# A transformer block on one core: side transfers on GpSimd's queue, and a first norm that spreads repeated columns into two banks

## The chip, the cores and the metric

The kernel runs on one NeuronCore of a Trainium2 chip. The metric is the device time of one execution in microseconds. Each core has a tensor engine (TensorE) for matrix products, a vector engine (VectorE), a scalar engine (ScalarE), GpSimd and SyncE; every engine takes its own instructions in order and waits on semaphores. Transfers between memory (DRAM) and the on-chip buffer (SBUF) run on 16 DMA engines; an instruction on SyncE, ScalarE or GpSimd issues them. TensorE writes to PSUM banks, which VectorE and ScalarE read.

## The reference

One block over 512 tokens of 1024 features, all in float32. A vector c gives six vectors of 1024 (adaLN) through a matrix `w_mod`:

```python
mod = (c_act @ w_mod[l] + b_mod[l])[:, None, :]        # c_act = silu(c)
shift_m, scale_m, gate_m, shift_f, scale_f, gate_f = jnp.split(mod, 6, axis=-1)
h = rms_norm(x, norm_mix[l]) * (1.0 + scale_m) + shift_m
z = h @ w_in[l]
qa, ka, va, xr, yr, qc, kc, vc, g_logits = jnp.split(z, IN_OFFSETS, axis=-1)
... # o_a: sliding-window attention, 8 heads; o_b: a gated linear recurrence (RG-LRU) times gelu(yr);
... # o_c: block-sparse attention (MoBA), 8 heads; both attentions add a bias by distance
merged = g[:, :, 0] * (o_a @ wb_a) + g[:, :, 1] * (o_b @ wb_b) + g[:, :, 2] * (o_c @ wb_c)
x = x + gate_m * (merged @ w_out[l])
h = rms_norm(x, norm_ffn[l]) * (1.0 + scale_f) + shift_f
u_gate, u_val = jnp.split(causal_dwconv(h @ w_up[l], ...), 2, axis=-1)
x = x + gate_f * ((jax.nn.silu(u_gate) * u_val) @ w_down[l])
```

## The kernel before

Features lie on the partitions: x is eight tiles of 128 features x 512 tokens (`X[0..7]`). Every large product is made in three passes of a reduced float32 format (float32r): a number is split into a high part and the exact rest, and high x high, high x low and low x high are added up (`mm3`). Weights arrive in chunks of 128x1024 (512 KB) in three buffers `raw`; ScalarE writes the high parts into `hi`, VectorE the rest into `lo` (`split`). TensorE then takes 24 products of a chunk.

The program is recorded, not issued at once. `Emitter` keeps, for each engine, a list of the instructions in the order of the code; `flush` (line 269) issues them at the end by a rough clock of its own. Up to the last of the first eight projections every engine's order is exactly the recorded one; behind that point each engine takes, among its next few instructions (`WINDOW`, line 49), the first whose operands the rough clock calls ready. The list `ORDER` (line 56) fixes the order of the later projections; between them TensorE takes up steps of side tasks: norms of heads, transposes, scores, the recurrence. Waits are put in from the operands. What is fixed at build time is each engine's order; if data come later than the rough clock thought, the engine waits there.

The prologue (lines 513 to 735). SyncE's queue loads `c8` and `CS` (c and an identity), the eight tiles of x, a table `V`, then w_mod and weights (`load_wm`, line 605; `stream_to`). TensorE spreads c over all partitions: for each half VectorE writes four diagonal blocks, and `spread` (line 593) multiplies them by ones. ScalarE squares the tiles of x, VectorE adds seven of them up; `token_ssq` (line 570) sums over the features by products with a column of ones, which gives a token per partition. `warm` (line 631) issues products whose result nobody reads. `rsqrt_sqrt` (line 576) makes the inverse root by a root on ScalarE and one Newton step on VectorE; `spread_diag` (line 586) writes its diagonals, half on each of the two engines, and two products by ones put 1/rms of all tokens on every partition, in one bank `rbk`. `mod_col` (line 609) makes a column of an adaLN vector: 128 features, the dot product of w_mod's rows with c on VectorE. `norm_in` (line 685) then makes h: for tile 0 from the bank, in two halves of the tokens, for the others from a copy `rb` in SBUF; the high part is written by ScalarE (`Hh`), the rest by VectorE (`Hl`). The first eight projections run f = 0..7 over the tiles of h, into eight banks at once.

Later, SyncE's queue carries everything else as well: rows of the attention bias out to DRAM and a tile for each head back (`bias_rows`, line 748; `bias_tile`, line 763), copies of k to the other half of the partitions (`turn_task`, line 803), 32 loads of w_mod (`mod_task`, line 998), gate weights (line 1055), gates out to DRAM and back (lines 1157, 1205), and x once more (`x_task`, line 1183). An instruction that waits in a queue holds all that is behind it. A weight load waits until the buffer `raw` that it fills has been split. `lru_task` (line 1065) writes the first column of a tile by a memset on GpSimd.

Of the kernel before, what the change touches and what calls it, by code (L numbers as in the profile page):

```python
# [10 lines left out]
F32 = mybir.dt.float32  # L11
# [3 lines left out]
OP = mybir.AluOpType  # L15
AX = mybir.AxisListType

S = 512
# [7 lines left out]
# Columns of the per-feature vectors ("vec" input): feature f of a vector sits at partition f % 128,  # L26
# column f // 128 of its range.
# [8 lines left out]
# Columns of the shape-only constants ("cst" input).  # L36
# [7 lines left out]
# from the end of an instruction to the start of one that needs it  # L44
DELAY = {("pe", "pe"): 0.0, ("act", "act"): 0.13, ("dve", "dve"): 0.13, ("act", "dve"): 0.145, ("act", "pe"): 0.27,
         ("dve", "act"): 0.14, ("dve", "pe"): 0.256, ("pe", "act"): 0.197, ("pe", "dve"): 0.2}
# What steers the order of issue. WINDOW: how many instructions of an engine are looked at; SLACK: how much later
# than the first ready one a longer one may start, in us; NEAR, BACKLOG, LIMIT: when the side tasks' steps are taken up.
WINDOW = {"pe": 160, "act": 45, "dve": 45, "dma": 6, "pool": 4}
SLACK, NEAR, BACKLOG, LIMIT = 1.2, 2, 8, 2  # L50
# how many heads are in flight, and how many up-projections start on the first half of the tokens
FLY, FIRST = 4, 5
# The order of the projections: qk, vc, xr, yr; m: the rest of the adaLN vectors may start; g, h: a branch's gates
# ahead of their use (swa, moba); a, b, c: the branches (swa, rg-lru, moba) into the merge. "-": no side tasks in
# between.
# [5 lines left out]
class Buf:  # L61
    """A tile that is used again and again; Tile orders its uses, the emitter picks the ones that are free."""
# [21 lines left out]
class Emitter:  # L84
    """Emits instructions engine by engine and keeps a rough clock of each engine, so that the tensor engine's
    stream takes up work of the side tasks when its operands are there. The order it picks is one of many right
    ones: Tile puts in every wait."""
# [15 lines left out]
    # clocks  # L103
    @staticmethod
    def keys(ap):
        """What an operand touches: the tile, or the 256 columns of a slot."""
# [73 lines left out]
    # instructions  # L180
# [68 lines left out]
    def sums(self, out, a):  # L249
        """out[:, h] = the sum of a[:, h, :]."""  # L250
        self._go("dve", 0.067 + self.n(a) * 0.00104, [out], [a], lambda: self.nc.vector.tensor_reduce(
            out, a, axis=AX.X, op=OP.add))
# [10 lines left out]
    def dma(self, out, in_, kb=256):  # L263
        self._go("dma", kb / 370, [out], [in_], lambda: self.nc.sync.dma_start(out, in_))  # L264
        for k in self.keys(out):
            self.w[k] += 2.0

    # the order of issue
# [1226 lines left out]
```

## Time and profile before

| what | value |
|---|---|
| time, median of 3 runs | 905.96 us (905.86 to 906.26) |
| profiled execution, first to last instruction | 904.7 us |
| TensorE busy | 895.8 us (99%) |
| VectorE busy | 630.1 us (70%) |
| ScalarE busy | 475.3 us (53%) |
| GpSimd busy | 1.8 us (0%) |
| DMA, mean over the span | 146 GB/s, 131.70 MB, all program transfers on one queue |

The profile is of one execution; its rows are times from the span's start. "PE" is TensorE, "PEld" its loads of weights, "DVE" VectorE, "ACT" ScalarE, "POOL" GpSimd, "SP" SyncE. Matrix products are pipelined and their ends are modelled, so that busy time alone does not tell whether TensorE is at its best rate; the distance from one start to the next does. A float32 product shows as two records. A line number is that of the helper which records the operation (L187 is every product, L213 every ScalarE operation), so that groups are told apart by the names of their tiles.

### The profile page before, as it was taken

What the parts mean: (1) busy time and instruction counts of PE and PEld (TensorE: products, weight loads), DVE (VectorE), ACT (ScalarE), POOL (GpSimd) and SP (SyncE); (2) the same over time, 40 slices, a digit from 0 to 9 for tenths busy, and PEclk for the clock granted to TensorE, in tenths of its full rate; (3) what the DMA queues carried; (4) which work ended last, traced back from release to release, by engine and by line L of the source; (5) the groups of instructions that cost most, each with busy time, mean ns of one, the idle gap of its engine ahead of it and who ended that gap; (6) DMA issues with size and microseconds to landing.
All of it is one profiled execution on the core that took longest, in us unless ns stands there. A gap on an engine that the chain in (4) does not pass through costs nothing.

```text
span 904.7 us, 12494 instructions
## 1 busy us (share of the span) xinstructions
PE 895.8 (99%) x4730; PEld 772.0 (85%) x4730; DVE 630.1 (70%) x1138; ACT 475.3 (53%) x763; POOL 1.8 (0%) x15
## 2 busy tenths in 40 slices
PE   7999999999999999999999999999999999999998
PEld 6889989889888888878888999888888888888888
DVE  6989989997876875887676888766656665522321
ACT  5366767985875898732223566544444444321110
POOL 0000000000000000000000000000000000000000
PEclk9999999999999999999999999999999999999999
DMA  8933532442254244586667655333222223333320
GB/s 315 347 119 99 155 99 93 129 163 95 73 172 155 90 140 152 184 275 214 229 226 285 213 173 172 123 101 107 97 93 93 93 97 103 104 116 105 117 82 24
DMA packets 44286, 131.70 MB, mean 146 GB/s; under 512 B 5393, under 2 KB 6937, under 8 KB 44226
## 3 DMA queue, kind: packets, MB, share of 16 engines
q1 hardware_dynamic: 44226, 130.90, 43.2%
q8 instruction: 37, 0.61, 0.3%
q14 instruction: 23, 0.19, 0.1%
HBM read 122.46 MB, written 5.80 MB: 142 GB/s over the span
## 4 chain that ended last, share of the span: by engine, by line
PE 93%; ACT 3%; DVE 2%; issue 1%; DMA 0%; SPq 0%; POOLq 0%; POOL 0%; ACTq 0%
PE bank L187 91%; PE bank L191 2%; ACT pair L213 2%; ACT L213 1%; DMA pair<-in_xT_dram 0%; DVE pair L243 0%; DVE pair L240 0%; DVE pair L246 0%; DVE lo L240 0%; ACT hi L213 0%; ACT rslot L213 0%; DVE rslot L240 0%; DVE pair L258 0%; SPq L264 0%; DVE rslot L243 0%
## 5 line engine op out<-in xcount | busy, mean ns | idle before, releaser
L187 PE MATMUL bank<-rslot,hi 128*128 128x512 f32 (+1 forms) x2332 | 656.8, 367 | 0.4 <-ACT rslot L213 0.4
L187 PEld LDWEIGHTS bank<-rslot,hi 128*128 128x128 f32 x2332 | 419.7, 189 | 70.1 <-ACT rslot L213 0.8
L187 PE MATMUL bank<-rslot,lo 128*128 128x512 f32 (+1 forms) x1166 | 427.0, 367 | 0.0
L240 DVE TENSOR_TENSOR lo<-raw,hi 128x1024 fp32r<-128x1024 f32 (+1 forms) x169 | 197.7, 1171 | 151.7 <-ACT hi L213 150.3
L213 ACT ACTIVATE hi<-raw 128x1024 fp32r<-128x1024 f32 (+1 forms) x153 | 156.6, 1025 | 185.3 <-PE bank L187 164.1
L187 PEld LDWEIGHTS bank<-rslot,lo 128*128 128x128 f32 x1166 | 219.9, 189 | 35.8
L187 PE MATMUL bank<-hi,rslot 128*128 128x256 f32 (+1 forms) x448 | 92.0, 315 | 0.1
L243 DVE SCALAR_TENSOR_TENSOR pair<-bank,V,pair 128x511 f32<-128x511 f32 (+2 forms) x112 | 83.6, 746 | 2.8 <-ACT pair L213 1.1
L187 PEld LDWEIGHTS bank<-hi,rslot 128*128 128x128 f32 x448 | 74.3, 190 | 6.3 <-issue 0.9
L213 ACT ACTIVATE rslot<-pair 128x512 fp32r<-128x512 f32 (+2 forms) x60 | 37.2, 622 | 76.7 <-DVE pair L240 72.6
L246 DVE CUSTOM_DVE_ANT_0 pair<-pair,pair,V 128x1024 f32<-128x1024 f32 x48 | 61.1, 1280 | 11.5 <-DMA pair<-in_wm_dram 11.5
L213 ACT ACTIVATE pair<-bank,V 128x512 f32<-128x512 f32 (+1 forms) x84 | 61.5, 732 | 4.8 <-PE bank L187 4.1
L213 ACT ACTIVATE pair<-bank 128x512 f32<-128x512 f32 (+2 forms) x75 | 43.2, 611 | 39.2 <-PE bank L187 38.6
L187 PE MATMUL bank<-lo,rslot 128*128 128x256 f32 (+1 forms) x224 | 62.5, 315 | 0.0
L213 ACT ACTIVATE pair<-pair 128x512 f32<-128x512 f32 (+1 forms) x62 | 35.2, 572 | 47.1 <-DVE pair L243 45.2
L240 DVE TENSOR_TENSOR rslot<-pair,rslot 128x512 fp32r<-128x512 f32 (+2 forms) x67 | 45.5, 680 | 15.2 <-ACT rslot L213 14.7
L240 DVE TENSOR_TENSOR pair<-pair,pair 128x512 f32<-128x512 f32 (+1 forms) x72 | 45.6, 636 | 12.6 <-ACT pair L213 7.6
L213 ACT ACT_TABLE_LOAD x37 | 47.5, 1283 | 5.2 <-PE bank L187 3.8
L187 PE MATMUL bank<-rslot,rslot 128*128 128x256 f32 (+3 forms) x288 | 48.8, 309 | 0.0
L187 PEld LDWEIGHTS bank<-rslot,rslot 128*128 128x128 f32 x288 | 43.4, 189 | 4.7 <-DVE rslot L240 0.8
L213 ACT ACTIVATE pair<-pair,small 128x256 f32<-128x256 f32 (+3 forms) x78 | 40.4, 529 | 11.3 <-DVE small L234 10.3
L187 PEld LDWEIGHTS bank<-lo,rslot 128*128 128x128 f32 x224 | 42.7, 190 | 2.6
(76 smaller groups left out, 412.5 us busy)
## 6 DMA issues: line engine op xcount, KB each, us to landing
raw<-in_wz_dram SPq DMA_DIRECT2D x50, 512.0 KB, 3.8
raw<-in_wup_dram SPq DMA_DIRECT2D x49, 512.0 KB, 3.3
pair<-in_wm_dram SPq DMA_DIRECT2D x48, 512.0 KB, 5.5
raw<-in_wdn_dram SPq DMA_DIRECT2D x22, 512.0 KB, 3.3
raw<-in_wout_dram SPq DMA_DIRECT2D x16, 512.0 KB, 3.3
pair<-in_xT_dram SPq DMA_DIRECT2D x16, 256.0 KB, 5.4
raw<-in_w_dram SPq DMA_DIRECT2D x8, 512.0 KB, 5.5
raw<-in_wbr_dram SPq DMA_DIRECT2D x16, 256.0 KB, 3.0
```

Source lines behind the costliest of these rows:

```text
L187: self._go("pe", cost, [out], [lhsT, rhs], lambda: self.nc.tensor.matmul(out, lhsT, rhs, start=start, stop=stop), rows=lhsT.shape[0] / 128)
L191: self._go("pe", 0.107, [out], [in_, ident], lambda: self.nc.tensor.transpose(out, in_, ident))
L213: self._go("act", c, outs, ins, lambda: self.nc.scalar.activation(out, in_, func, scale=scale, **kw), "tanh" if func == AF.Tanh else t)
L240: self._dve([out], [a, b], lambda: self.nc.vector.tensor_tensor(out, a, b, op=op))
L243: self._dve([out], [a, s, b], lambda: self.nc.vector.scalar_tensor_tensor(out, a, s, b, op0=op0, op1=op1))
L246: self._dve([out, accum], [a, b, s], lambda: self.nc.vector.tensor_tensor_reduce(out, a, b, 1.0, s, op0, op1, accum_out=accum))
```

## The change

Seen from the code, there are three parts. First, queues: `dma` can issue from ScalarE, which the two small tables at the start do, and a new `side` issues from GpSimd, with a cost of its own in the rough clock. It is used for the bias rows and tiles, the copies of k, the 32 loads of w_mod and the vector c they need, the gate weights, the gates out and back, and the late x. Weights, the first x and the outputs stay with SyncE. The memset of the recurrence moves to VectorE. Second, the prologue: c and 1/rms are spread by products that take a column, repeated 128 times, as weights and the identity as the other operand, so that no diagonals are written; 1/rms goes into two banks, two blocks of tokens each. Squares are shared between ScalarE (five) and VectorE (three); the sum over the features begins with the first six tiles; the warm products are 6, 2, 6 and 6 instead of 7, 6 and 6. Third, orders in the prologue: the rest of the table `V` and the store of c behind the second tile's w_mod, the low half of h ahead of that of the weights, the two gains `gq` behind them. Comments are taken out as well, which the diff below leaves away.

```diff
-    def dma(self, out, in_, kb=256):
-        self._go("dma", kb / 370, [out], [in_], lambda: self.nc.sync.dma_start(out, in_))
+    def dma(self, out, in_, kb=256, act=False):
+        if act:
+            self._go("act", 0.4, [out], [in_], lambda: self.nc.scalar.dma_start(out, in_))
+        else:
+            self._go("dma", kb / 370, [out], [in_], lambda: self.nc.sync.dma_start(out, in_))
...
+    def side(self, out, in_, kb=256):
+        self._go("pool", 0.9, [out], [in_], lambda: self.nc.gpsimd.dma_start(out, in_), table=kb / 370)
+        for k in self.keys(out):
+            self.w[k] += 2.0
...
+            if e == "pool" and op[5]:
+                moved = max(t + 1.5, moved) + op[5]
+                end[i] = moved + 0.9
...
-    E.dma(c8, cvec, 4)
-    E.dma(CS, cst, 66)
+    E.dma(c8, cvec, 4, act=True)
+    E.dma(CS, cst, 66, act=True)
...
+    def spread_cols(bk, cols, nb):
+        for i in range(nb):
+            E.mm(blk(bk.ap, i), cols[:, i:i + 1].to_broadcast([128, 128]), ident, True, True)
...
-    E.dma(V[:, NEARLY:], vec[:, NEARLY:], 130)
...
-        dg = E.slot()
-        for j in range(4):
-            E.ts(blk(dg.ap, j), ident, c8[:, 4 * i + j:4 * i + j + 1], None, OP.mult)
-        spread(cb[i], 4, dg.ap)
-        E.drop(dg)
...
+        spread_cols(cb[i], c8[:, 4 * i:4 * i + 4], 4)
...
-    E.act(sq.ap, X[0].ap, AF.Square)
-    for k in range(1, KT):
-        s1 = E.slot()
-        E.act(s1.ap, X[k].ap, AF.Square)
-        if k < KT - 1:
-            E.tt(sq.ap, sq.ap, s1.ap, OP.add)
-            E.drop(s1)
+    sq = [E.slot() for _ in range(4)]
+    for k in range(KT):
+        t = sq[0 if k == 0 else 3 if k == 7 else 1 + k % 2]
+        if k in (0, 2, 7):
+            E.tt(t.ap, X[k].ap, X[k].ap, OP.mult)
+        else:
+            E.act(t.ap, X[k].ap, AF.Square)
         if k in (3, 5):
             E.act(cp[k // 2 - 1].ap, cb[k // 2 - 1].ap, AF.Copy)
-    warm(7)
-    token_ssq(bk, s1.ap, 0, 4, True, False)
-    token_ssq(bk, sq.ap, 0, 4, False, True)
+        if 0 < k < 6:
+            E.tt(sq[0].ap, sq[0].ap, t.ap, OP.add)
     warm(6)
-    E.drop(*cb, sq, s1)
-    d_c = dr.tile([1, D], F32, name="dc")[:]
-    E.dma(d_c, cp[0].whole[0:1, :], 4)
+    token_ssq(bk, sq[0].ap, 0, 4, True, False)
+    E.tt(sq[3].ap, sq[3].ap, sq[1].ap, OP.add)
+    warm(2)
+    token_ssq(bk, sq[3].ap, 0, 4, False, True)
+    warm(6)
+    E.drop(*cb, *sq)
     for i in (1, 0):
         load_wm(1, i)
     stream_to(2, 0)
-    E.ts(gq[:, 0:1], v("qa"), 0.125, None, OP.mult)
-    E.ts(gq[:, 1:2], v("qc"), 0.125, None, OP.mult)
+    E.dma(V[:, NEARLY:], vec[:, NEARLY:], 130)
+    d_c = dr.tile([1, D], F32, name="dc")[:]
+    E.dma(d_c, cp[0].whole[0:1, :], 4)
...
-    spread_diag(rs, 4, dg.ap)
     E.drop(bk)
-    rbk, rb = E.bank(), E.slot()
-    for cs in halves:
-        E.mm(rbk.ap[:, cs], ones, dg.ap[:, cs], True, True)
+    rbk, rb = [E.bank(), E.bank()], E.slot()
+    for i in range(2):
+        spread_cols(rbk[i], rs[:, 2 * i:2 * i + 2], 2)
     warm(6)
...
-    norm_in(0, rb=rbk)
+    norm_in(0)
+    norm_in(0, True)
     E.tt(los[0], raws[0], his[0].bitcast(F32), OP.subtract)
     Stream.split = 1
-    norm_in(0, True)
-    E.act(rb.ap, rbk.ap, AF.Copy)
-    E.drop(rbk)
+    for i in range(2):
+        E.act(rb.ap[:, halves[i]], rbk[i].ap[:, 0:256], AF.Copy)
+    E.drop(*rbk)
+    E.ts(gq[:, 0:1], v("qa"), 0.125, None, OP.mult)
+    E.ts(gq[:, 1:2], v("qc"), 0.125, None, OP.mult)
...
-        E.dma(out, bass.AP(tensor=src.tensor, offset=src.offset + h * w, ap=[[1, 128], [1, n]]), n / 2)
+        E.side(out, bass.AP(tensor=src.tensor, offset=src.offset + h * w, ap=[[1, 128], [1, n]]), n / 2)
...
-                E.dma(h.ap[o], h.ap[p], 128)
-                E.dma(l.ap[o], l.ap[p], 128)
+                E.side(h.ap[o], h.ap[p], 128)
+                E.side(l.ap[o], l.ap[p], 128)
...
-            E.dma(raw[i][0].whole, wm[16 + i], 512)
+            E.side(raw[i][0].whole, wm[16 + i], 512)
...
-        E.memset(th.ap[:, 0:1], 1.0)
+        E._dve([th.ap[:, 0:1]], [], lambda: nc.vector.memset(th.ap[:, 0:1], 1.0))
...
-            E.dma(g.ap, d_g[b, t])
+            E.side(g.ap, d_g[b, t])
...
-            E.dma(XR[k].ap, xT[k])
+            E.side(XR[k].ap, xT[k])
...
-            E.dma(d_g[b, t], g.ap)
+            E.side(d_g[b, t], g.ap)
```

## Rows read from the trace of the kernel before

**Rows 1.** The page, busy time of each engine, share of the span, instructions:

```profile
PE 895.8 (99%) x4730; PEld 772.0 (85%) x4730; DVE 630.1 (70%) x1138; ACT 475.3 (53%) x763; POOL 1.8 (0%) x15
```

**Rows 2.** TensorE's waits, the whole span: us in total, times, longest:

```profile
PE bank L187 <- DVE pair L234: 4.3, 1, 4.3
PE bank L187 <- ACT pair L213: 1.0, 1, 1.0
PE bank L187 <- ACT rslot L213: 0.4, 1, 0.4
```

**Rows 3.** TensorE by stretch: from:to, length, busy (records), granted clock, DMA share, GB/s:

```profile
700.00:740.00 40.00, 40.00 (x178) 1.00 0.28 92
```

**Rows 4.** Timeline of SyncE's queue: start, us, operation, count:

```profile
0.73 0.39 SPq L264 DMA_DIRECT2D c<-in_cvec_dram  x1
...
1.65 3.74 SPq L264 DMA_DIRECT2D pair<-in_xT_dram  x8
```

**Rows 5.** Timeline of ScalarE: first and last squares of a run of eight operations:

```profile
6.99 1.24 ACT L213 ACTIVATE pair<-pair 128x512 f32<-128x512 f32 x2 [1.13 <-DMA pair<-in_xT_dram]
...
10.18 1.14 ACT L213 ACTIVATE pair<-pair 128x512 f32<-128x512 f32 x2
```

**Rows 6.** Timeline of TensorE: from the sums to the first projection; at 387 us:

```profile
11.37 2.17 PE L187 MATMUL bank<-ones,pair 128*128 128x1 f32 x16 [0.98 <-ACT pair L213]
13.41 2.91 PE L187 MATMUL bank<-ones 128*128 128x128 f32 x12
16.11 1.16 PE L187 MATMUL bank<-pair,ones 128*128 128x256 f32 x4
17.10 1.50 PE L187 MATMUL bank<-ones 128*128 128x128 f32 x12
18.38 3.91 PE L187 MATMUL bank<-hi,rslot 128*128 128x512 f32 x16
...
387.41 0.50 PE L187 MATMUL bank<-rslot,hi 128*128 128x512 f32 x1 [0.38 <-ACT rslot L213]
```

**Rows 7.** Timeline of VectorE: additions, column sum, Newton step, norm, low half, column sum:

```profile
10.06 1.49 DVE L240 TENSOR_TENSOR pair<-pair,pair 128x512 f32<-128x512 f32 x2
...
11.84 1.29 DVE L246 CUSTOM_DVE_ANT_0 pair<-pair,pair,V 128x1024 f32<-128x1024 f32 x1 [0.16 <-DMA pair<-in_wm_dram]
...
14.49 0.16 DVE L243 SCALAR_TENSOR_TENSOR small<-small,small 128x4 f32<-128x4 f32 x1
...
17.30 0.87 DVE L243 SCALAR_TENSOR_TENSOR pair<-pair,small,bank 128x256 f32<-128x256 f32 x2 [0.93 <-PE bank L187]
18.09 1.22 DVE L240 TENSOR_TENSOR lo<-raw,hi 128x1024 fp32r<-128x1024 f32 x1
...
20.02 1.28 DVE L246 CUSTOM_DVE_ANT_0 pair<-pair,pair,V 128x1024 f32<-128x1024 f32 x1
```

**Rows 8.** The same by stretch, all five engines (PE, PEld, DVE, ACT, POOL):

```profile
14.00:16.00 2.00, 2.00 (x11) 2.00 (x11) 1.90 (x8) 1.26 (x3) 0.00 (x0) 0.50 0.89 352
16.00:18.00 2.00, 2.00 (x15) 1.90 (x15) 1.07 (x4) 0.57 (x2) 0.00 (x0) 0.91 1.02 369
```

**Rows 9.** Timeline: ScalarE's halves of the first norm; TensorE at the second projection:

```profile
17.82 0.91 ACT L213 ACTIVATE rslot<-pair,small 128x256 fp32r<-128x256 f32 x2 [1.43 <-DVE pair L243]
...
24.18 3.52 PEld L187 LDWEIGHTS bank<-hi,rslot 128*128 128x128 f32 x16 [0.50 <-ACT rslot L213]
```

**Rows 10.** SyncE's waits, the longest in total, the whole span:

```profile
SPq L264 <- DVE lo L240: 502.6, 136, 8.0
```

**Rows 11.** Tiles `pair` on GpSimd, who waited for its memsets: us, times:

```profile
  DVE pair L240: 3.7, 3
```

**Rows 12.** DMA issues, copies of k: count, KB each, median us to landing:

```profile
rslot<-rslot SPq DMA_DIRECT2D x20, 128.0 KB, 2.2
```

**Rows 13.** Tile `dmoba`, last line: landings of the eight MoBA bias tiles:

```profile
DMA to landing us min/median/max: 3.0/4.1/4.4
```

**Rows 14.** VectorE by form, one group: count, busy, mean ns, idle before:

```profile
L234 DVE TENSOR_SCALAR pair<-pair,small 128x256 f32<-128x256 f32 x25 | 8.1, 346 | 0.0
```

More of the change, by code (lines that the diff above doesn't have):

```diff
@@ L622, in hybrid_trunk_kernel @@
     for i in range(2):
-        dg = E.slot()
-        for j in range(4):
-            E.ts(blk(dg.ap, j), ident, c8[:, 4 * i + j:4 * i + j + 1], None, OP.mult)
-        spread(cb[i], 4, dg.ap)
-        E.drop(dg)
-    bk = E.bank()
-    sq, wb = E.slot(), E.bank()
+        spread_cols(cb[i], c8[:, 4 * i:4 * i + 4], 4)
+    bk, wb = E.bank(), E.bank()
     def warm(n):
@@ L661, in hybrid_trunk_kernel @@
     rsqrt_sqrt(rs, st, bk.ap[:, 0:4], 4)
-    dg = E.slot()
-    spread_diag(rs, 4, dg.ap)
     E.drop(bk)
-    rbk, rb = E.bank(), E.slot()
-    for cs in halves:
-        E.mm(rbk.ap[:, cs], ones, dg.ap[:, cs], True, True)
+    rbk, rb = [E.bank(), E.bank()], E.slot()
+    for i in range(2):
+        spread_cols(rbk[i], rs[:, 2 * i:2 * i + 2], 2)
     warm(6)
-    E.drop(dg, wb)
+    E.drop(wb)
     E.act(his[0], raws[0], AF.Copy)
@@ L683, in mod_in, with norm_in @@
             load_wm(f + 2, i)
-    def norm_in(f, low=False, rb=rb):
-        for cs in halves if f < 1 else (slice(0, S),):
+    def norm_in(f, low=False):
+        for i, cs in enumerate(halves if f < 1 else (slice(0, S),)):
             if low:
@@ L689, in norm_in @@
             else:
-                E.stt(X[f].ap[:, cs], X[f].ap[:, cs], scs[f][:, 1:2], rb.ap[:, cs], OP.mult, OP.mult)
+                E.stt(X[f].ap[:, cs], X[f].ap[:, cs], scs[f][:, 1:2], rbk[i].ap[:, 0:256] if f < 1 else rb.ap, OP.mult,
+                      OP.mult)
                 E.act(Hh[f].r[:, cs], X[f].ap[:, cs], AF.Identity, bias=scs[f][:, 0:1])
@@ L755, in bias_rows @@
         E.drop(bk, hot)
-        E.dma(d_swa, b.ap[0:8, 0:384], 12)
-        E.dma(d_moba[:, 0:127], b.ap[0:8, 0:127], 4)
-        E.dma(d_moba[:, 127:639], a.ap[8:16, :], 16)
+        E.side(d_swa, b.ap[0:8, 0:384], 12)
+        E.side(d_moba[:, 0:127], b.ap[0:8, 0:127], 4)
+        E.side(d_moba[:, 127:639], a.ap[8:16, :], 16)
         E.drop(a, b)
@@ L1000, in mod_task @@
         c2 = E.pair()
-        E.dma(c2[0].whole, bass.AP(tensor=d_c.tensor, offset=d_c.offset, ap=[[0, 128], [1, D]]), 512)
+        E.side(c2[0].whole, bass.AP(tensor=d_c.tensor, offset=d_c.offset, ap=[[0, 128], [1, D]]), 512)
         raw = []
@@ L1056, in gate_weights @@
         raw, h, l = E.slot(), E.rslot(), E.rslot()
-        E.dma(raw.ap, wgate[s])
+        E.side(raw.ap, wgate[s])
         yield Need(aps=(raw.ap,))
```

## The prediction, written before the change was run

> **What bounds the kernel now.** I read the page first: TensorE is busy for 895.8 of 904.7 us, VectorE 70%, ScalarE 53%, GpSimd not at all [rows 1]. Such a share can hide stalls, so next come TensorE's waits: there are three, 4.3 us at the start, 1.0 us in the prologue and 0.4 us at 387 us [rows 2, 6]. Then the rate: of the stretches of 40 us from 300 us on, ten hold the same 178 records, 0.2247 us each; one of the ten stands in [rows 3]. From the first projection on, TensorE is the bound and is fed; its work is the same after the change (the 128x128 records of the prologue apart). So the time is the start of the projections plus fixed work, and there are two places for a gain: the prologue of 24 us and what is left of waits behind it, 0.4 us as records show it.
>
> The prologue is read from the timeline of its engines. The loads of x are issued from 1.65 us on, behind two small tables [rows 4]. ScalarE squares all eight tiles of x and copies two banks; its last eight operations run from 6.99 to 11.32 us, 0.54 us apart [rows 5]. TensorE sums them over the features in 16 records (a float32 matmul shows as two), 11.37 to 13.54 us; then 12 records that only keep it warm, then four that spread the result, and the first projection at 18.38 us [rows 6]. Between sums and spread lie the root, a Newton step that ends at 14.65 us, and diagonals written by both engines [rows 7]. The granted clock is 0.50 from 14 to 16 us and between that and 1.00 in the slices beside it [rows 8]: TensorE had just been idle or busy with one-column products. That clock matters: 12 warm records take 2.70 us there (13.41 to 16.11) and 1.28 us at full clock (17.10 to 18.38) [rows 6], and the spread stands behind them in TensorE's queue.
>
> The second projection (tile 1 of h) starts at 24.18 us, on ScalarE's half of the norm, released by VectorE [rows 9]. VectorE's queue, not TensorE, sets this point: 24 records at 0.2247 would have ended at 18.38 + 5.39 = 23.77 us. From there TensorE has work until the end, so the moment that counts is 24.18.
>
> **The change part by part.** The sum is made against the profiled execution's 904.7 us; the median of the runs, 905.96, is 1.26 us more, and I carry that over.
>
> *Loads.* The two tables go to ScalarE's queue, so x is issued at 0.73 instead of 1.65 us: 0.92 us earlier. The tables (68 KB) still share the DMA engines, so I take 0.85 (bounds 0 and 0.92). The two issues hold ScalarE for about 0.4 us each [rows 4]; its squares then begin at about 4.65 us, when x1 has just landed. This costs nothing.
>
> *Sums of squares.* ScalarE keeps five squares; VectorE takes three and six additions, 0.75 us apart or less [rows 7]. With x 0.85 us earlier, ScalarE squares x3 at 6.77 and, at 0.54 us a step, x5 at 8.39, done at 9.0, and x6 by 10.1. VectorE's addition of x5 waits for its own queue and ends at 10.0, the square of x7 at 10.65, the last addition at 11.4. That is no earlier than ScalarE's 11.32 now; but the products for the first sum are done by then, and 8 records remain instead of 16: 11.45 to 12.55 instead of 13.54 us. Gain 1.0 us.
>
> *Root and Newton step.* Unchanged operations: from 13.58 to 14.65 now, 12.6 to 13.65 then. The column sum that VectorE does beforehand takes 1.48 us from 11.84 [rows 7]; it now starts behind the last addition at 11.4 and ends at 12.9, just before the step needs VectorE. If that addition is 0.3 us later, so is everything after it.
>
> *Spread.* Removed: four diagonals, two on each engine, and the hop behind them. Added: eight records that take a column repeated 128 times as weights. No such weights are in the trace; the nearest rows are the 128-column records with plain ones, 0.11 us at full and 0.22 us at half clock, so eight cost 0.9 or 1.8 us (now: four of 256 columns, 1.0 us across the change of clock). I see no reason for more. But they stand behind 12 warm records that can begin only when the sums are done, at 12.55 us. At full clock these end at 13.85, the spread at 14.75; the norm then waits for VectorE's other column sum (1.28 us from 13.6) and starts at 14.9 instead of 17.30: 2.4 us earlier. With a half-clock stretch from 13 to 16.4 us as now, the warm records end at 14.45, the first bank is readable at 15.5 (1.8 us earlier), the second only at 16.4.
>
> *Order behind the norm.* Now VectorE goes from the norm (17.30) over the low half of the first weights (18.09) and of h to the next column sum at 20.02: 2.72 us [rows 7]. The change puts the low half of h ahead of that of the weights, so it waits for ScalarE (0.5 us a half [rows 9]), and moves two small operations on the gains (0.21 us) behind it: 0.87 for the norm, 0.23 of waiting, 0.93 for the low half of h, 1.2 for that of the weights and 0.2 make 3.45 us, 0.7 us lost. From that column sum to the second projection remain 4.16 us.
>
> *Sum of the prologue.* Full clock: 14.9 + 3.45 + 4.16 = 22.5 by these rows, or 22.2 as the starts overlap: 1.7 to 2.0 us gained. Half clock as now: 15.5, 0.3 us more for the late second bank, then 23.3: 0.9 us gained. TensorE itself is no bound in either (its warm records end at 16.0 or 17.6 and 5.39 us of projection follow). Which clock? TensorE's work before is thinner than now: its early warm records end sooner against the sums, and the sums are one-column products again. So I take half clock, 0.9.
>
> *Side transfers.* About 110 transfers leave SyncE's queue for GpSimd's. SyncE waited 502.6 us for the low halves of weights [rows 10], and what stood behind such a load waited too; yet TensorE stalled 0.4 us. The stall moved away is therefore worth 0 to 0.4 us. The stretch around 387 us also has the memset on GpSimd between ScalarE and VectorE; VectorE waited 3.7 us for it in three places [rows 11], and it is now VectorE's own. I take 0.3 us for both. The trace holds no transfer issued by GpSimd; its 15 instructions are memsets. On SyncE a copy of k lands after 2.2 us [rows 12], a bias tile of the eight MoBA heads after 3.0 to 4.4 [rows 13]; the price on GpSimd is bounded by zero (a queue without weights in front) and by some tenths of a microsecond each. The cover is the projections that TensorE takes up in between. What queues on GpSimd behind one waiting transfer is now other side transfers, no longer weights.
>
> VectorE has operations with one float32 input in SBUF, 25 of them 346 ns long on 128x256 [rows 14]; today nothing stands beside them on GpSimd. An issue on GpSimd that had to wait for one of them would be late by that much, which is the step the third rival is built on. The Trainium skill (SBUF — State Buffer, Who interferes with whom) says that a VectorE operation in a two-port mode, such as a float32 copy from SBUF to SBUF, locks GpSimd out of the ports it writes descriptors through until it ends. This rule speaks against the change; no run here shows it yet.
>
> 905.96 - 0.9 - 0.3 = 904.76, say 904.8.
>
> **The rivals.** *A: the clock does not fall between sums and projections.* For it: the three groups of warm records are spread anew (6, 2, 6, 6 products instead of 7, 6, 6). Against it: the sums still need 2 us of one-column products with a pause ahead. Then 1.7 to 2.0 + 0.3 us: 903.8.
>
> *B: the half-clock stretch comes earlier, under the sums, or lasts into the last warm records.* Sums at 0.21 us a record cost 0.9 us more than at 0.11, the 12 last warm records 1.3 us more. The gain is eaten: 905.5 to 906.5, 906.0. For it: TensorE has nothing to do from about 8 to 10 us.
>
> *C: side transfers come late, and TensorE waits for them.* 16 bias tiles and five groups of k copies, 21 in all, go straight into the scores of a head, and TensorE takes its records in a fixed order. If each landed one VectorE operation later (0.35 us [rows 14]) and half of it reached TensorE, that is 21 x 0.35 / 2 = 3.7 us, less the 1.2 gained: 908.5, slower. It decides from the point where a lateness exceeds what lies between the landing and the record; against it speaks that TensorE shows no wait at all between 24 and 387 us although those landings on SyncE differ by 1.4 us [rows 2, 13].
>
> *D: the queue was no obstacle and the loads start no earlier* (the DMA engines and not the issue set them): half of the prologue's gain goes, 905.4. It lies within the forecast's own range.
>
> **How the numbers follow.** A measurement of this kernel can tell about 0.2%, 1.8 us, from no change: faster means under 904.15, slower over 907.77. Half clock as now, with D in it: 0.50, 904.0 to 905.7. A: 0.27, 903.3 to 904.3. B: 0.10. C: 0.13. Faster: 0.85 of A and a sixth of the first, 0.31. Slower: 0.11 of C and 0.02 of B, 0.13. Within: 0.56. The range 903.4 to 907.0 leaves out most of C above and the best of A below.
>
> **What would show it.** Right: x issued at 0.7 us; eight sum records ending near 12.5; the second projection at 23.3 (22.2 under A) and 178 records in 40 us afterwards; no wait of TensorE above 0.5 us behind it. Wrong: waits of TensorE on scores or transposes between 60 and 250 us (C); warm or spread records at 0.21 us next to the first projection (B); spread records above 0.22 us each; more than 1.3 us around the span, which no row bounds, because two more queues must be set up and drained.

## The result, and the profile after the change

The changed kernel takes **911.58 us** (median of five executions, 911.33 to 912.69) against 905.96 before: a ratio of 1.0058 (95% interval 1.0046 to 1.0070). It is 5.6 us slower, where the prediction gave 904.8 and a range up to 907.0. The profiled execution took 912.69 us, its span is 910.9.

In some executions TensorE's granted clock falls to 0.50 for 3.4 us before the first projection [rows 8], in others it doesn't. Of 19 executions of the kernel before that ran beside the first four experiments, eight kept the clock (mean over the span 0.999 or more, called "at full clock" below; median 905.1 us) and ten lost it once (0.998; 906.3 us). So a difference under 1.5 us is read among like executions. Of the changed kernel four of five kept the clock (911.6 us); the profiled one did not, nor did that of the kernel before.

The busy shares on the page of the changed kernel answer to [rows 1]:

```profile
PE 898.3 (99%) x4748; PEld 774.1 (85%) x4748; DVE 628.6 (69%) x1132; ACT 480.3 (53%) x766; POOL 61.4 (7%) x119
```

TensorE's and VectorE's hardly differ, ScalarE has 5.0 us more, and GpSimd's 7% is the issuing of transfers. TensorE's waits answer to [rows 2] (us in total, times, longest):

```profile
PE bank L187 <- DMA CS<-in_cst_dram: 4.7, 1, 4.7
PE bank L187 <- DVE rslot L240: 1.7, 5, 0.8
PE bank L191 <- DVE pair L234: 1.4, 1, 1.4
PE bank L187 <- ACT rslot L213: 0.9, 1, 0.9
```

The last three lines lie where the kernel before has no wait: at 182 to 207 us, and 0.2 us at 334. Transposes of probabilities wait for VectorE's scaling (1.4), scores and products for halves of operands. The view by stretches of 10 us shows that place (from:to, length, busy time of PE, PEld, DVE, ACT, POOL, granted clock, DMA share, GB/s; the sum is that of the seven stretches from 150 to 220 us):

```profile
180.00:190.00 10.00, 9.78 (x55) 8.38 (x53) 9.07 (x25) 8.57 (x13) 2.72 (x5) 1.00 0.69 198
190.00:200.00 10.00, 7.51 (x39) 5.78 (x38) 8.43 (x28) 8.97 (x28) 1.09 (x2) 1.00 0.39 106
200.00:210.00 10.00, 8.85 (x60) 7.41 (x59) 9.80 (x36) 9.90 (x26) 0.56 (x1) 1.00 0.11 26
...
sum 70.00, PE 66.14 PEld 57.16 DVE 57.97 ACT 64.32 POOL 9.17; mean PE 9.45 PEld 8.17 DVE 8.28 ACT 9.19 POOL 1.31
```

TensorE loses 3.9 us in 30, and ScalarE is busy for 64.3 of the 70 us. In the kernel before it is 59.2 of 70, and TensorE has no gap there:

```profile
sum 70.00, PE 70.00 PEld 61.93 DVE 60.38 ACT 59.21 POOL 0.20; mean PE 10.00 PEld 8.85 DVE 8.63 ACT 8.46 POOL 0.03
```

The groups of ScalarE in the same 70 us name a part of the difference (count, busy, mean ns, idle before), first of the changed kernel, then of the one before:

```profile
L213 ACT ACTIVATE pair<-pair,small 128x256 f32<-128x256 f32 (+3 forms) x33 | 18.4, 562 | 1.8 <-DVE small L255 1.8
L213 ACT ACT_TABLE_LOAD x7 | 9.0, 1283 | 0.1
...
L213 ACT ACTIVATE pair<-pair,small 128x256 f32<-128x256 f32 (+3 forms) x28 | 15.6, 571 | 4.2 <-DVE small L234 3.2 <-DVE small L255 1.0
L213 ACT ACT_TABLE_LOAD x4 | 5.1, 1283 | 0.1
```

Seven table loads (ACT_TABLE_LOAD, 1.28 us each, where ScalarE goes over to another kind of function) stand where the kernel before has four, and 33 exponentials and scalings of heads where it has 28. Both kernels have 37 table loads in all. So heads and the switches between function tables have been moved together, until ScalarE bounds that stretch: of the chain of work that ended last, 61% from 163 to 208 us is ScalarE's and 21% TensorE's.

The side transfers themselves are hardly later (the view of issues: count, KB each, median us from issue to landing), against 2.2 us in [rows 12] and 4.1 in [rows 13]:

```profile
rslot<-rslot POOLq DMA_DIRECT2D x20, 128.0 KB, 2.5
pair<-dmoba POOLq DMA_DIRECT2D x8, 256.0 KB, 4.4
```

The start answers to [rows 5 to 7]. In the timeline of VectorE (start, length, operation, count), the first addition, the last square and the last addition:

```profile
6.10 0.69 DVE L240 TENSOR_TENSOR pair<-pair,pair 128x512 f32<-128x512 f32 x1 [1.77 <-ACT pair L213]
...
10.42 0.68 DVE L240 TENSOR_TENSOR pair<-pair 128x512 f32<-128x512 f32 x1
11.21 0.69 DVE L240 TENSOR_TENSOR pair<-pair,pair 128x512 f32<-128x512 f32 x1
```

In that of ScalarE, the second table load, a root behind it and the first square:

```profile
4.05 1.28 ACT L213 ACT_TABLE_LOAD   x1
5.34 0.20 ACT L213 ACTIVATE junk<-epsc 128x1 f32<-128x1 f32 x1
5.45 0.61 ACT L213 ACTIVATE pair<-pair 128x512 f32<-128x512 f32 x1
```

In that of TensorE, the second half of the sums, fillers (the products of `warm`), spread, fillers and the first projection:

```profile
12.00 1.01 PE L187 MATMUL bank<-ones,pair 128*128 128x1 f32 x8
12.87 2.63 PE L187 MATMUL bank<-ones 128*128 128x128 f32 x12
15.29 1.68 PE L187 MATMUL bank<-CS,small 128*128 128x128 f32 x8
16.81 1.50 PE L187 MATMUL bank<-ones 128*128 128x128 f32 x12
18.07 1.17 PE L187 MATMUL bank<-hi,rslot 128*128 128x512 f32 x4
```

Everything from the sums to the norm is later than predicted. The clock falls at 13.2 us (its mean in the slice below is 0.59), and from there the records of 128 columns take 0.21 us each:

```profile
13.00:14.00 1.00, 1.00 (x7) 1.00 (x7) 0.85 (x8) 0.95 (x2) 0.00 (x0) 0.59 1.01 393
```

The second projection starts at 23.89 us; before it was 24.18 [rows 9].

### The profile page after: what moved, and what is told of

Its sections match the earlier page's. It is cut to its first block, busy times and chain, and to the rows that moved or that the text cites. A ratio compares the mean times of both kernels' runs of the same rounds, so it can differ in the third digit from the quotient of the medians.

```text
span 910.9 us, 12543 instructions
## 1 busy us (share of the span) xinstructions
PE 898.3 (99%) x4748; PEld 774.1 (85%) x4748; DVE 628.6 (69%) x1132; ACT 480.3 (53%) x766; POOL 61.4 (7%) x119
## 4 chain that ended last, share of the span: by engine, by line
PE 88%; ACT 6%; DVE 3%; issue 1%; DMA 1%; DVEq 0%; POOLq 0%; ACTq 0%
PE bank L187 87%; ACT pair L213 3%; PE bank L191 2%; ACT L213 1%; ACT rslot L213 1%; DVE pair L240 1%; ACT hi L213 1%; DVE pair L243 1%; DVE rslot L240 0%; DVE lo L240 0%; DVE pair L246 0%; DMA c<-in_cvec_dram 0%; DMA pair<-in_wgate_dram 0%; DVE pair L258 0%; DVE rslot L230 0%
## 5 line engine op out<-in xcount | busy, mean ns | idle before, releaser
L213 ACT ACTIVATE hi<-raw 128x1024 fp32r<-128x1024 f32 (+1 forms) x157 | 161.8, 1032 | 193.4 <-PE bank L187 175.8
L213 ACT ACTIVATE rslot<-pair 128x512 fp32r<-128x512 f32 (+2 forms) x64 | 39.7, 622 | 79.9 <-DVE pair L240 67.9
L213 ACT ACTIVATE pair<-bank 128x512 f32<-128x512 f32 (+3 forms) x76 | 43.1, 604 | 32.6 <-PE bank L187 31.7
L213 ACT ACTIVATE pair<-pair 128x512 f32<-128x512 f32 (+1 forms) x59 | 33.3, 569 | 47.0 <-DVE pair L243 45.6
L187 PE MATMUL bank<-rslot,rslot 128*128 128x256 f32 (+3 forms) x288 | 51.2, 313 | 2.7 <-DVE rslot L240 1.7
```

What stands on the lines that cost most here:

```text
L187: self._go("pe", cost, [out], [lhsT, rhs], lambda: self.nc.tensor.matmul(out, lhsT, rhs, start=start, stop=stop), rows=lhsT.shape[0] / 128)
L213: self._go("act", c, outs, ins, lambda: self.nc.scalar.activation(out, in_, func, scale=scale, **kw), "tanh" if func == AF.Tanh else t)
```

## The experiments

**Plan or queue.** The change does two things to a side transfer: another engine issues it, and the kernel's planner books it on another clock. `_go` books every operation on a first clock, from which it is decided when a task (a head, a gate) is taken up; `flush` then orders the records on a second. The theory is that the *order* costs; the rivals are that the *queue* costs, or the new prologue. Four kernels separate them. The first undoes all of `side`:

```diff
     def side(self, out, in_, kb=256):
-        self._go("pool", 0.9, [out], [in_], lambda: self.nc.gpsimd.dma_start(out, in_), table=kb / 370)
+        self._go("dma", kb / 370, [out], [in_], lambda: self.nc.sync.dma_start(out, in_))
```

> The new prologue alone: the twelve side transfers are put back on SyncE's queue and on SyncE's clock in the planner, everything else is as in the changed kernel. Order theory (the planner's clock for the side transfers gave another order of work, which lets TensorE wait at 181 to 207 us): the stalls of that stretch are gone, second projection at 23.9 us, 905.5 us (905 to 906.5). Queue theory (transfers through GpSimd cost by themselves): the same 905.5 us. Prologue theory (the new prologue shifts the planner's clocks and that alone brings the stalls): 910 to 912 us.

The second keeps that booking and lets GpSimd issue; the third keeps the booking of the changed kernel and lets SyncE issue. TensorE, ScalarE and VectorE get the same records in the same order as in the first kernel and in the changed one respectively.

```diff
-        self._go("dma", kb / 370, [out], [in_], lambda: self.nc.sync.dma_start(out, in_))
+        self._go("dma", kb / 370, [out], [in_], lambda: self.nc.gpsimd.dma_start(out, in_))
...
-        self._go("pool", 0.9, [out], [in_], lambda: self.nc.gpsimd.dma_start(out, in_), table=kb / 370)
+        self._go("pool", 0.9, [out], [in_], lambda: self.nc.sync.dma_start(out, in_), table=kb / 370)
```

> The order of work of the kernel with the new prologue alone on TensorE, ScalarE and VectorE, record for record, but the twelve side transfers are issued by GpSimd. Order theory: what that kernel takes, within 0.5 us (905 to 906.5). Queue theory: 909 to 912 us, with TensorE waits at the heads.

> The order of work of the changed kernel on TensorE, ScalarE and VectorE, record for record, but the twelve side transfers are issued by SyncE among the weight loads. Order theory: 910 to 912 us, with the same TensorE waits at 181 to 207 us. Queue theory: 905 to 906.5 us, without them.

Measured, median of all executions and, behind it, at full clock:

| side transfers booked on | issued by SyncE | issued by GpSimd |
|---|---|---|
| SyncE's clock | 905.44 / 905.4 | 906.40 / 906.3 |
| GpSimd's clock | 910.22 / 910.2 | 911.58 / 911.6 (the change) |

Down a column only the order differs: 4.9 and 5.2 us. Along a row only the queue: 1.0 and 1.3 us. The new prologue alone is 0.3 us slower than the kernel before, at full clock (905.4 against 905.1) and where the clock falls (906.55 against 906.3). The order theory holds for most of it, the queue for the rest. The first kernel (new prologue, all on SyncE), the sum over the same 70 us:

```profile
sum 70.00, PE 69.95 PEld 61.75 DVE 60.05 ACT 58.10 POOL 0.00; mean PE 9.99 PEld 8.82 DVE 8.58 ACT 8.30 POOL 0.00
```

Its table loads in this stretch, by groups:

```profile
L213 ACT ACT_TABLE_LOAD x3 | 3.8, 1283 | 0.1
```

The third kernel (booked as in the change, all on SyncE), the same sum:

```profile
sum 70.00, PE 66.14 PEld 57.38 DVE 57.52 ACT 63.95 POOL 0.00; mean PE 9.45 PEld 8.20 DVE 8.22 ACT 9.14 POOL 0.00
```

With not one transfer on GpSimd, TensorE loses the same 3.86 us in the same stretch, and ScalarE has the same 64 us of work in it, with seven table loads. The first kernel has three of them and a gap of 0.05 us.

That place holds the whole cost of the order. Worked out from the starts in the two traces, against the median distance from one record of a form to the next in the first kernel, TensorE loses 6.6 us between 180 and 210 us in the third kernel and 0.8 in the first. The views show 3.9 and 0.05 of these as waits; the rest is hidden in records that count as busy. Of the 5.8 us more, 1.0 comes back at 553 us, where only the first kernel waits.

**The old prologue with the new side transfers** (diff: the prologue of before, `side` as in the change).

> The side transfers alone: the prologue of the kernel before, with the twelve side transfers on GpSimd's clock and queue and the one-column memset on VectorE as in the changed kernel. Order theory: the time depends on the order that comes out of the planner; it need not be that of the changed kernel, 906 to 912 us, and TensorE's waits lie wherever ScalarE's work gathers. Queue theory: 909 to 912 us. Prologue theory: 906 us.

914.16 us, above every range expected, with TensorE's waits at 184 to 208 us, 1.4 us longest again. So the new prologue doesn't bring them. It is worse than the change itself by 2.6 us. In all four executions the mean clock was 0.994 or 0.996, and a part of the 2.6 is that: in the profiled one it is 0.50 for 6.8 us in the prologue and for 3.4 us at 201 us, behind the first waits (one fall of 3.4 us costs 1.2).

**What in the booking does it.** On the first clock GpSimd's transfers stand in line: one that waits for its data holds back those recorded behind it. There a gate that is stored at 188.8 and copies of k at 200.9 hold the bias tile of the first MoBA head, which counts as landed at 207.4 in place of 198.6; of two window heads it counts as landed 2.8 and 1.9 us later. (These are the planner's times, not the chip's.) The first test takes only that line away:

```diff
+        c = self.clk["pool"]
+        self.clk["pool"] = 0.0
         self._go("pool", 0.9, [out], [in_], lambda: self.nc.gpsimd.dma_start(out, in_), table=kb / 370)
+        self.clk["pool"] = c
```

> The changed kernel, but in the planner's first clock a side transfer no longer waits for the ones recorded before it on GpSimd (it still waits for its own data). No operation is added or taken away; the queue stays GpSimd's. Order theory (the in-order clock made the planner take up the heads 4 to 9 us late): the waits of TensorE at 181 to 207 us go, 906 to 907 us, as in the kernel with SyncE's clock and GpSimd's queue. Rival (any order made with the new flush costs for GpSimd brings them): 909 to 912 us.

> The same order of work as the run before on TensorE, ScalarE and VectorE, with the side transfers issued by SyncE. If GpSimd's queue costs 1.0 to 1.3 us by itself, as the two pairs so far say, this is 1.0 to 1.3 us below the run before: 904.5 to 905.5 us. If those differences belonged to their orders, the two are alike.

907.88 us on GpSimd's queue (907.6 at full clock) and 906.04 on SyncE's (905.7). The stalls at 182 to 207 us are gone but for one of 0.6 us, so without the line on the planner's clock they don't arise. That the line does more than any other shift of that clock would, one kernel can't show; hence the next two. The first expectation was about 1 us too low, the second 0.5: the queue costs 1.9 us in this order, not 1.0 to 1.3.

The converse: everything on SyncE, and the planner alone is told that two tiles land later.

```diff
         bias_tile(T.ap[:, :wid], d_swa if swa else d_moba, hd, wid)
+        if swa and hd in (3, 7):
+            for x in E.keys(T.ap[:, :wid]):
+                E.w[x] += 2.77 if hd == 3 else 1.94
```

> The kernel with the new prologue and everything on SyncE (905.4 us), with one thing changed: the planner is told that the bias tiles of two of the eight window heads (3 and 7) land 2.8 and 1.9 us later than it thought, which is by how much the clock of GpSimd had put them later. Nothing on the chip is later. Order theory: stalls of TensorE come back around 160 to 250 us, 912 us or more. Rival (the stalls need the transfers on the other queue, or the whole new clock): 905 to 906.5 us.

**927.15 us**: 21.7 us more, from two numbers in a table. TensorE now waits in ten places from 215 to 250 us (and 0.4 us at 181), and once for 5 us at 512 us, for the high parts of weights, which ScalarE writes late (two of its waits):

```profile
PE bank L187 <- ACT hi L213: 5.5, 2, 5.0
PE bank L191 <- DVE pair L234: 1.7, 1, 1.7
```

Does it take late bias tiles, or does any small shift do?

```diff
-SLACK, NEAR, BACKLOG, LIMIT = 1.2, 2, 8, 2
+SLACK, NEAR, BACKLOG, LIMIT = 1.2, 1.95, 8, 2
```

> The kernel with the new prologue and everything on SyncE (905.4 us), with one constant of the planner changed by a fortieth: NEAR, how far ahead of TensorE's clock a task's data may be when it is taken up, 1.95 us in place of 2. No transfer, operation or wait is added. Order theory in its wide form (the recorded order sits on an edge, and any small shift of the planner's clocks can move heads together): some 8 to 16 us slower, 913 to 921 us, with TensorE waits between 160 and 220 us and near 500 us. Narrow form (only late bias tiles of heads do it): 905 to 907 us.

920.44 us, the wide form. Again heads at 177 to 202 us and late high parts at 504 us:

```profile
PE bank L187 <- ACT hi L213: 7.0, 2, 5.6
PE bank L191 <- DVE pair L234: 2.2, 1, 2.2
```

The long wait has another cause than the heads. ScalarE is not late with the high parts: the weights are. It waits 10.88 us for them here (its timeline), and 10.31 us in the kernel before this one:

```profile
508.42 1.06 ACT L213 ACTIVATE hi<-raw 128x1024 fp32r<-128x1024 f32 x1 [10.88 <-DMA raw<-in_wout_dram]
```

Their load stands in SyncE's queue behind side transfers that wait for VectorE to free their buffers, the longest for 10.2 us here (a tile of x) and for 9.0 us there (a column of w_mod). And the clock falls with these waits. It is 0.50 for 3.4 us from 202 and for 10.2 us from 506 us here, and for 6.8 us from 223 and from 516 us there; two slices of this kernel (granted clock behind the busy times):

```profile
500.00:510.00 10.00, 4.38 (x35) 4.18 (x33) 7.90 (x13) 1.06 (x1) 0.00 (x0) 0.80 0.76 254
510.00:520.00 10.00, 8.65 (x55) 8.36 (x55) 9.25 (x15) 5.01 (x8) 0.00 (x0) 0.69 0.79 304
```

So the 15 and the 21.7 us are heads that gather, a queue that one waiting transfer blocks, and the clock; how much is whose was not taken apart.

It is no property of side transfers, then: 0.05 us in one constant of the planner is enough to leave the good order. Not every shift is: the changes to the prologue below and the free clock above keep TensorE nearly as full as before.

**What the queue costs.** In the order with the free clock, only the small transfers (bias rows and tiles, copies of k) stay on GpSimd:

```diff
+        small = in_.tensor.name[:4] in ("rslo", "dswa", "dmob") or out.tensor.name[:4] in ("dswa", "dmob")
+        q = self.nc.gpsimd if small else self.nc.sync
```

> The order of work of the two kernels with the free planner clock; of the side transfers only the small ones (bias rows and tiles, copies of k) are issued by GpSimd, the large ones (adaLN columns, gates, gate weights, late x) by SyncE. Tail theory (GpSimd's queue costs 0.4 us at the end, for more semaphores that SyncE reads one after the other, and the rest of its 2 us comes from large loads that land later and that VectorE waits for): 0.4 us over the kernel with all on SyncE (905.7 us at full clock), so 906.1 us. Rival (the small ones, with a head waiting for each, are what costs): 907 to 907.8 us.

905.66 us (905.6 at full clock, and all ten executions kept the clock), below both expectations: the small ones, 39 issues, cost nothing that the time shows, though the span ends 0.3 us later behind TensorE's last record (3.52 us, against 3.19 with all on SyncE). The large ones cost the 2 us. They are not slower as a rule: the columns of w_mod land after 5.0 us in the middle with either queue. Single ones are, up to 7.6 us against 6.8. One place shows how. With two queues, in the kernel with the large ones on GpSimd too: a column of w_mod issued at 495.96 us by GpSimd and weights issued at 496.87 by SyncE (the view of issues; the last number is us to landing):

```profile
pair<-in_wm_dram POOLq DMA_DIRECT2D x1, 512.0 KB, 6.8
raw<-in_wout_dram SPq DMA_DIRECT2D x1, 512.0 KB, 6.1
```

With one queue, in the kernel with the small ones alone on GpSimd, the same pair, issued by SyncE at 494.56 and 495.69 us:

```profile
pair<-in_wm_dram SPq DMA_DIRECT2D x1, 512.0 KB, 4.3
raw<-in_wout_dram SPq DMA_DIRECT2D x1, 512.0 KB, 5.2
```

In one queue the column, issued first, lands first (498.9 us, the weights 500.9). From two they land together (502.8 and 503.0). What follows there, in the timeline of VectorE:

```profile
502.93 1.28 DVE L246 CUSTOM_DVE_ANT_0 pair<-pair,pair,V 128x1024 f32<-128x1024 f32 x1 [2.49 <-DMA pair<-in_wm_dram]
```

And in TensorE's waits:

```profile
PE bank L187 <- DVE lo L240: 0.8, 1, 0.8
```

VectorE waits 2.49 us for the column, and TensorE 0.8 us for the low half of the next weights, which stands behind it in VectorE's queue. Record for record, the two traces drift apart by 1.0 us at this place, by 0.6 at 328 us and by 0.2 between 369 and 387; elsewhere they run level.

**The prologue: where the tables are issued.**

```diff
-    E.dma(c8, cvec, 4, act=True)
-    E.dma(CS, cst, 66, act=True)
+    E.dma(c8, cvec, 4)
+    E.dma(CS, cst, 66)
```

> The kernel with the new prologue and everything on SyncE (905.4 us), with the two small loads of the start (c and the table) issued by SyncE ahead of x again, as before the change; the order of work is the same but for the first 20 records. Late-c theory (c lands at 3.8 us because it shares the DMA engines with x, and this takes back the earlier x): c lands near 2.3 us, x 0.9 us later, the second projection within 0.4 us of 22.3 us at full clock, time within 0.5 us. Load theory (x decides): second projection 0.8 us later, 906.2 us.

907.94 us, and the load theory was right about x: its last tile lands at 10.76 us in place of 9.65, and c at 2.33 helps nothing. But neither theory had foreseen the larger effect. In none of ten executions did the clock stay up (six at 0.998, 906.9 us; four lower). TensorE has spread c early, and then nothing to do for 2.9 us ahead of the sums (timeline of TensorE):

```profile
7.04 1.55 PE L187 MATMUL bank<-ones 128*128 128x128 f32 x12
11.49 1.05 PE L187 MATMUL bank<-ones,pair 128*128 128x1 f32 x8 [2.90 <-DVE pair L240]
...
13.80 2.77 PE L187 MATMUL bank<-ones 128*128 128x128 f32 x12
```

That it is this idle time that brings the fall was not tested by itself.

**The prologue: the order on VectorE.** The swap that the prediction priced at 0.7 us, undone:

```diff
-    norm_in(0, True)
     E.tt(los[0], raws[0], his[0].bitcast(F32), OP.subtract)
     Stream.split = 1
+    norm_in(0, True)
```

> The kernel with the new prologue and everything on SyncE (905.3 us at full clock), with one pair swapped back behind the first norm: the low part of the first weights ahead of the low halves of the activations on VectorE. The prediction priced this order at 0.7 us. By that the second projection comes 0.7 us earlier (21.6 us at full clock) and the time is 904.6 us. Rival (VectorE works without a pause from 14 us to the second projection, so the swap moves nothing behind both): within 0.2 us of 905.3 us.

905.07 us; at full clock 905.0 against 905.4, the second projection at 22.27 in place of 22.50 us. Both expectations missed: 0.3, not 0.7 and not 0. TensorE waits 0.08 us there instead of 0.35, and then its own first projection, which ends at 22.19, is the bound. Against the kernel before, this version is at 0.9987 (0.9977 to 0.9997): nine of twelve executions kept the clock, where three of the 23 of before beside it did. At full clock the two are level.

**The prologue: the additions.** Three squares summed by TensorE instead of added by VectorE, with fillers between the products:

```diff
-        if 0 < k < 6:
+        if 0 < k < 5:
             E.tt(sq[0].ap, sq[0].ap, t.ap, OP.add)
-    warm(6)
+    warm(4)
     token_ssq(bk, sq[0].ap, 0, 4, True, False)
-    E.tt(sq[3].ap, sq[3].ap, sq[1].ap, OP.add)
+    warm(2)
+    token_ssq(bk, sq[2].ap, 0, 4, False, False)
+    warm(2)
+    token_ssq(bk, sq[1].ap, 0, 4, False, False)
     warm(2)
     token_ssq(bk, sq[3].ap, 0, 4, False, True)
-    warm(6)
+    warm(12)
```

> The kernel with the new prologue and everything on SyncE (905.3 us at full clock), with three of the eight squares no longer added on VectorE but summed by TensorE, each by four one-column products. VectorE theory (its chain of additions to 11.9 us sets the sums and so the norm): the last sum ends at 11 us instead of 13.0, the first projection starts 0.9 us earlier, the second at 21.5 us, time 904.4 us. Rival (the loads of the adaLN columns and of the first weights set it): the first projection no earlier than now less 0.3 us, 905 to 905.3 us.

911.85 us, and no answer to the question: the fillers that were to keep the clock up stand on the path themselves. The timeline of TensorE from the last sum on:

```profile
14.60 1.71 PE L187 MATMUL bank<-ones,pair 128*128 128x1 f32 x8
16.17 5.15 PE L187 MATMUL bank<-ones 128*128 128x128 f32 x24
21.15 1.06 PE L187 MATMUL bank<-CS,small 128*128 128x128 f32 x8
```

From a group of eight sum records to what follows it are 0.82 us at full clock, so four groups without fillers would have lasted from 10.04 to about 13.5 us (an estimate), against 13.0 with the additions: no gain was to be had this way. Then the clock fell, at 14.0 us, and 24 filler records took 5.15 us. With fewer of them, in the version with the swap undone:

```diff
     token_ssq(bk, sq[3].ap, 0, 4, False, True)
-    warm(6)
+    warm(2)
```

> The kernel with the low part of the weights first (905.05 us at full clock, 906.3 us where the clock falls in the start), with two filler products in place of six between the sums of squares and the spread. Filler theory (at half clock the twelve filler records hold the spread back by 1.1 us, at full clock by 0.2): 905.4 us where the clock falls, 904.9 us where it does not. Rival (fewer fillers let the clock fall in more executions, or longer): most executions at the lower clock and 906 us or more.

905.44 us: 905.0 at full clock, 906.1 where it falls (expected 905.4), and it fell in six of twelve. The fillers don't hold the spread back any more (it starts at 14.30 us in an execution that lost the clock), but the clock now falls under the spread and the second group of fillers, and the time is spent there. The rival is nearer.

## Why the prediction was wrong, step by step

*Bound.* TensorE is full from the first projection on, and where no head waits its rate is unchanged. But the conclusion, that the time is the start of the projections plus fixed work and that only this start and 0.4 us of waits can move, takes the order of the records for given. It is made by a planner whose booking the diff changes.

*Side transfers*, the step that failed. It costed an issue, a landing and a queue, took 0.3 us of gain, and put the new order at nothing without a reason. Measured are 4.9 to 5.2 us lost by the order, between 180 and 210 us, and 1.0 to 1.3 by the queue. The price that it set on the queue, zero to some tenths a transfer, was fair for the small ones (nothing that shows over 39 of them); it left out that a large one can land late beside another queue's, with VectorE waiting for it. That SyncE's queue holds back at most 0.4 us is true of the order before only: in two other orders weights came late behind side transfers, and TensorE waited 5.5 and 7.0 us for their high parts. The memset on VectorE was not tested alone.

*Issues on GpSimd.* GpSimd issued 112 transfers in 0.52 to 0.65 us each, 0.54 in the middle; none stands out by the 0.35 us of [rows 14], and the small ones moved alone cost no time that shows. By the Trainium skill (SBUF — State Buffer, Who interferes with whom) VectorE's two-port operations hold such issues up; no run here shows a cost of that.

*Loads.* Right in direction: x is issued at 0.75 us, and its last tile lands at 9.23 instead of 10.40 us, 1.17 us earlier (0.85 taken). Wrong in "this costs nothing": c, issued by ScalarE beside x, lands at 3.8 instead of 2.33 us, the second table load ends at 5.33, and the first square starts at 5.45 instead of 4.65.

*Sums.* The last addition ends at 11.9, not 11.4: VectorE's first addition waits 1.77 us for that late square, until 6.10, and from there VectorE works almost without a pause. The eight records end at 13.01, not 12.55: a gain of 0.5 us instead of 1.0. The *Newton step* follows (14.11 against 13.65).

*Spread.* The eight records take 0.21 us each at half clock, as bounded. The first bank is read at 16.39, not 15.5: 0.5 us come from the sums, 0.4 from the 12 fillers, which last to 15.5. The clock is not the surprise here, it falls at 13.2 us and was taken to fall at 13; the prediction's sum was short. At its own 0.11 and 0.22 us a record the fillers from 12.55 on would have ended at about 14.7, not 14.45, and begun later, more of them run at the lower clock.

*Order behind the norm.* From norm to column sum 3.34 us, predicted 3.45: right. Of the 0.6 us that it loses against the order before, the swap back gains only 0.3.

*Sum of the prologue.* The second projection at 23.89 (half clock, predicted 23.3) and, in the kernel with the new prologue alone, 22.50 (full clock, predicted 22.2). The gain is 0.3 us at half clock, and it is lost again behind: the order that comes with it has a wait of 0.6 us at 553 us in place of one of 0.4 at 387, and times where the clock falls are 0.3 us longer in the end.

*Rivals.* A came true as to the clock in four of five executions, not as to the time (903.8), and a clock kept more often is what the new prologue is worth: of ten executions with it alone seven kept the clock; of all 84 of the kernel before that ran beside the experiments, 21 did. It explains why the medians differ by 5.6 us and the times at full clock by 6.5. B did not show in the changed kernel. C named the place (heads, 60 to 250 us) and the sign, but not the cause: landings are 0.3 us later and SyncE's queue gives the same stalls, so that it forecast a slower kernel is luck. D fell: the loads did start earlier. Around the span lie 1.8 us, as in executions of the kernel before (the 1.26 us carried over set the median of the runs against the span of another execution); GpSimd's queue adds 0.4 us inside it, from TensorE's last record to the end (3.59 against 3.18 us in the two kernels booked on SyncE).

*Open.* Which of the heads' operations tips the stretch was not isolated: seven table loads instead of three are 5 us of ScalarE's 6, but no run changed them alone. What decides in one execution whether the clock falls isn't settled either. Nor is whether c lands late for the 256 KB loads beside it or for the other queue that it came by.

## What to carry to other kernels

Where a kernel computes its own order of issue, an edit to a cost, an engine's name or a due time is an edit to the whole program: compare the order of records per engine before costing anything, and test the plan and the queue apart, since they can be swapped one at a time. A second queue was no faster path for large transfers here, and a load issued first no longer landed well ahead of the next. One queue has its price too, when a transfer that waits for its buffer stands ahead of weights. A wait that the profile shows can be less than what an engine loses: compare starts with starts. Judge a microsecond only among executions whose clock did the same.

## What the runs showed of the hardware

- Two 512 KB loads issued about 1 us apart landed one after the other from one queue (4.3 and 5.2 us) and together from two (6.8 and 6.1 us); this is one pair, and over all late columns of w_mod the median is 5.0 us either way.
- A 4 KB load that ScalarE issued in the same moment as SyncE's 256 KB loads landed after 3.1 us, against 1.6 us when SyncE issued it ahead of them.
- In two kernels with one queue, side transfers that waited for their buffers, the longest 9.0 and 10.2 us, held the weight load behind them, and ScalarE waited 10.31 and 10.88 us for the weights.
- Where TensorE stood idle for 5.0 and 5.6 us in the middle of the program, its granted clock fell to 0.50 for 6.8 and 10.2 us. Behind waits of 1.4 and 0.9 us at about 200 us it fell for 3.4 us in one kernel (old prologue, new side transfers) and not in the changed one.
- GpSimd's queue, once used, made the end of the span 0.3 to 0.4 us longer (3.52 to 3.59 us from TensorE's last record, against 3.18 and 3.19).
- With the same records in the same order, TensorE's clock fell before the first projection in some executions and not in others (three of ten). It stayed up in 21 of 84 executions of the kernel before, and in none of ten where TensorE idled for 2.9 us ahead of the one-column sums.
